# Hybrid encoder block on one core: the feed-forward's first product in seven block products of eight, with the weight sums made in DRAM

## Chip, core and metric

The program runs on one core of one Trainium2 chip. The metric is the device time of one execution in microseconds (us), lower is better. TensorE (PE in the profile) multiplies, VectorE (DVE) and ScalarE (ACT) work elementwise, GpSimd (POOL) fills and masks small tiles, and SyncE (SP) issues the DMAs. Each engine works through its own list of instructions in the order in which the program was emitted.

## The reference, cut to what matters

One layer of a hybrid encoder over 16 + 512 positions with 1024 features: a normed projection, a convolution branch, a gated delta rule with 8 heads, and a feed-forward part. The change is in the feed-forward part alone:

```python
    u2 = rmsnorm(h, norm_ffn_w)
    up = causal_dwconv(u2 @ w_up, ffn_dw_w, ffn_dw_b)        # w_up: 1024 x 5632, three taps per channel
    f_gate, f_val = jnp.split(up, 2, axis=-1)                # 2816 channels each
    return h + (jax.nn.silu(f_gate) * f_val) @ w_down        # w_down: 2816 x 1024
```

## The kernel before

Activations lie with features on the 128 partitions and time along the row: 8 tiles of features, 516 time steps in the last stages. All large products are made in single-precision pieces: an operand x is split into a rounded part hi (ScalarE copies it into the type fp32r) and a rest lo (VectorE subtracts), and a product takes three terms, hi·hi, lo·hi and hi·lo. `weights` (line 449 on) brings one 128 x 1024 weight tile by DMA into one of three `wr` buffers, and splits it into `wh` and `wl`, two buffers each. `gemm` then issues, for 8 feature tiles, 3 terms and 2 halves of time, 48 matmuls of 258 columns into a PSUM tile of the pool `p2` (two buffers).

The program is recorded as a list of operations; `Plan.order` sorts them. It keeps one clock per engine, prices every operation (`price`, line 295), honours buffers (`SLOTS`) and picks for each engine the ready operation of the lowest priority number. `BIAS` shifts the priorities of named groups, `with plan.at(...)` applies them, so a change of the table changes every engine's order in the whole program. All instructions are issued by one line (459), which is why the rows of the profile differ by tile names and not by lines.

Stages in the order of time: projections and convolutions (`glu`), the decay masks of the delta rule (`decays`: a DMA, then an `affine_select` on GpSimd), the triangular inverses (`inverses`, tile `DU`), which `grow` (called for heads 0 to 3 and for heads 4 to 7) assembles into the matrices `Mn`: 16 small copies of diagonal blocks a call on ScalarE, zeros in `LL` from GpSimd, then small matmuls `gP` and `gX`. `heads` runs the recurrence; its `conv4` lets GpSimd clear four columns of a tile `ra` before ScalarE copies the accumulator there. Then the gated branch products (`y`), the output product (`wo`), the second norm, the feed-forward (`up`, `dn`), the final norm.

In the feed-forward, `up(t)` makes one of 44 channel tiles: 48 matmuls on the unnormed `hh`, `hl`, two VectorE multiplications with the norm's row `r` out of PSUM, and three taps (one ScalarE, two VectorE operations). Gate tile t goes through Silu, is multiplied with value tile t, and split into `fh[t]`, `fl[t]`, which the 8 products `dn` read. The residual `hs` stays in SBUF until `dn`.

## Time and profile before

| | |
|---|---|
| median of 3 runs | 1035.56 us (1034.06 to 1035.69) |
| the profiled execution | 1031.66 us, its span 1029.9 us |
| mean granted TensorE clock in it | 0.994 |
| TensorE busy | 1015.1 us, 99% of the span |
| VectorE, ScalarE, GpSimd busy | 717.1, 473.6 and 9.4 us |
| stretch of the product `up` | 639.8 to 894.8 us of the span |
| stretch of the product `dn` | 894.8 to 1010.3 us |

The profile follows one execution. "Busy" is the share of time in which an engine had an instruction under way; the chain of waits follows the last instruction back to whatever released each step; the table by stretches gives busy time, granted clock and DMA load between two times. The mean duration of an instruction contains a tail in which the engine already works at the next one: where starts stand in a row, the distance of two starts is what an instruction costs its engine.

### The profile page before, as it was taken

To read this page: it belongs to the slowest core of one execution; us is meant where nothing else is said; L and a number is where in the kernel's file an instruction comes from. 1 tells how busy PE (TensorE), PEld (TensorE's weight loads), DVE (VectorE), ACT (ScalarE), POOL (GpSimd) and SP (SyncE) were. 2 spreads that over 40 slices of the span, in tenths; PEclk is the share of its full clock that TensorE was granted. 3 is DMA by queue.
4 is the path that set the end of the run, shared out by engine and by line. 5 is a ranking of instruction groups with operands and counts; after the bars stand their busy time and mean duration, and the time that the engine had idled before them with its cause. 6 is when DMAs were issued, how large, how long until landed. Compare 5 with 4: busy or idle time off the path is not lost.

```text
span 1029.9 us, 20012 instructions
## 1 busy us (share of the span) xinstructions
PE 1015.1 (99%) x8430; PEld 973.8 (95%) x8430; DVE 717.1 (70%) x1237; ACT 473.6 (46%) x844; POOL 9.4 (1%) x45
## 2 busy tenths in 40 slices
PE   9998999999999999999999999999999999999996
PEld 7998999998999999999999999999999999988886
DVE  5987999999999999443565555666676767622334
ACT  6777713468545545444373334544434443422222
POOL 0000000000000000000000000000000000000000
PEclk9999999998999999999999999999999999999999
DMA  6243423241212133123214333222232222233332
GB/s 229 76 115 82 128 90 114 83 103 64 73 63 82 53 114 115 62 73 114 93 43 154 128 109 100 85 83 100 86 99 88 86 99 87 93 93 92 97 92 82
DMA packets 44042, 98.40 MB, mean 96 GB/s; under 512 B 12720, under 2 KB 19248, under 8 KB 43952
## 3 DMA queue, kind: packets, MB, share of 16 engines
q1 hardware_dynamic: 43952, 97.12, 29.5%
q8 instruction: 66, 1.08, 0.4%
q14 instruction: 24, 0.20, 0.1%
HBM read 93.89 MB, written 3.21 MB: 94 GB/s over the span
## 4 chain that ended last, share of the span: by engine, by line
PE 93%; DVE 4%; ACT 1%; DMA 1%; issue 0%; SPq 0%; DVEq 0%; ACTq 0%
PE up L459 25%; PE dn L459 12%; PE ga L459 9%; PE y L459 9%; PE q L459 5%; PE v L459 5%; PE z L459 5%; PE wo L459 5%; PE cv L459 4%; PE cg L459 4%; PE o L459 2%; DVE cv L459 1%; PE k L459 1%; PE rs L459 1%; PE S L459 1%; PE qk L459 1%
## 5 line engine op out<-in xcount | busy, mean ns | idle before, releaser
L459 DVE TENSOR_TENSOR wl<-wr,wh 128x1024 fp32r<-128x1024 f32 x157 | 189.2, 1206 | 154.3 <-PE dn L459 59.8
L459 ACT CAST wh<-wr 128x1024 fp32r<-128x1024 f32 x157 | 162.2, 1035 | 257.1 <-PE dn L459 58.2
L459 DVE SCALAR_TENSOR_TENSOR ca<-c,par,ca 128x516 f32<-128x516 f32 (+12 forms) x240 | 176.7, 745 | 3.7 <-ACT ca L459 1.0
L459 PE MATMUL up<-hl,wh 128*128 128x258 f32 x704 | 141.5, 282 | 0.0
L459 PE MATMUL up<-hh,wh 128*128 128x258 f32 x704 | 141.5, 282 | 0.0
L459 PEld LDWEIGHTS up<-hh,wh 128*128 128x128 f32 x704 | 109.2, 190 | 0.2 <-issue 0.2
L459 PEld LDWEIGHTS up<-hl,wh 128*128 128x128 f32 x704 | 108.7, 189 | 0.0
L459 PE MATMUL up<-hh,wl 128*128 128x258 f32 x704 | 92.3, 284 | 0.0
L459 PEld LDWEIGHTS up<-hh,wl 128*128 128x128 f32 x704 | 88.2, 190 | 0.0
L459 PE MATMUL dn<-fh,wh 128*128 128x512 f32 (+1 forms) x198 | 71.6, 370 | 0.0
L459 PE MATMUL dn<-fl,wh 128*128 128x512 f32 (+1 forms) x198 | 71.6, 370 | 0.0
L459 DVE SCALAR_TENSOR_TENSOR uy<-up,par,uy 128x512 f32<-128x512 f32 x88 | 65.9, 749 | 2.8 <-ACT uy L459 1.3
L459 DVE TENSOR_TENSOR up<-up,r 128x258 f32<-128x258 f32 x88 | 33.5, 420 | 47.4 <-PE up L459 44.6
L459 ACT ACTIVATE uy<-up,par 128x512 f32<-128x512 f32 x44 | 35.9, 817 | 55.8 <-DVE up L459 55.8
L459 PE MATMUL ga<-ul,wh 128*128 128x258 f32 (+1 forms) x256 | 58.0, 288 | 0.0
L459 PE MATMUL ga<-uh,wh 128*128 128x258 f32 (+1 forms) x256 | 57.2, 288 | 0.0
L459 DVE SCALAR_TENSOR_TENSOR cv<-ra,par,cv 128x528 f32<-128x528 f32 x69 | 51.7, 765 | 1.4 <-ACT cv L459 1.3
L459 PE MATMUL dn<-fh,wl 128*128 128x512 f32 (+1 forms) x198 | 45.4, 369 | 0.0
L459 PEld LDWEIGHTS dn<-fh,wh 128*128 128x128 f32 x198 | 37.2, 188 | 7.0
L459 PEld LDWEIGHTS dn<-fl,wh 128*128 128x128 f32 x198 | 37.2, 188 | 6.9
L459 PE MATMUL ga<-uh,wl 128*128 128x258 f32 (+1 forms) x256 | 43.1, 286 | 0.0
L459 PEld LDWEIGHTS ga<-ul,wh 128*128 128x128 f32 x256 | 42.2, 190 | 0.6 <-issue 0.4
(284 smaller groups left out, 2194.6 us busy)
## 6 DMA issues: line engine op xcount, KB each, us to landing
wr<-in_win SPq DMA_DIRECT2D x64, 512.0 KB, 3.4
wr<-in_wup SPq DMA_DIRECT2D x44, 512.0 KB, 3.4
wr<-in_wd SPq DMA_DIRECT2D x17, 512.0 KB, 3.5
wr<-in_wdn SPq DMA_DIRECT2D x8, 512.0 KB, 3.5
wr<-in_wco SPq DMA_DIRECT2D x8, 512.0 KB
wr<-in_wo SPq DMA_DIRECT2D x8, 512.0 KB, 3.4
wr<-in_wd SPq DMA_DIRECT2D x8, 384.0 KB, 3.5
x<-in_xT SPq DMA_DIRECT2D x8, 264.0 KB, 5.6
```

Source lines behind the costliest of these rows:

```text
L459: getattr(engines[o.eng], o.fn)(*(get(x) for x in o.a), **{n: get(x) for n, x in o.k.items()})
```

## The change

The 22 gate and 22 value tiles are paired. The first three pairs (`NPRE`) go the old way, 48 matmuls a tile. For the other 19 pairs, the weights of a pair are a 2 x 2 matrix of blocks (even and odd feature tiles by gate and value), the activations a 2 x 2 matrix (even and odd feature tiles by first and second half of time), and `seven` makes the product in seven block products of 12 matmuls each instead of eight. The seven are accumulated into two PSUM tiles of the pool `p1` (four buffers), `sx` and `sz`, in turn; after each product the running sum is read out: `quarters` does this with four ScalarE and three VectorE operations of 258 columns a pair.

The blocks' sums: for the activations `factors` builds them once, on VectorE and ScalarE, right after the second norm, from normed tiles `xn`, in four groups (`nh`, `nl`, `nhl` are their split parts); three more block tiles than before have to be held, so `hs` is written to DRAM (`d_h`) and read back in `dn` (`back`). For the weights `presums` makes the four sums of every pair in DRAM (`ws`): five DMAs a pair issued by GpSimd, two plain copies and three that add to what is there, each group waiting for what it adds to; the first is held behind the last decay mask, and a pair behind the pair two before. A pair's weights are then 3.5 tiles of 128 x 1024 instead of 2.

Beside that: the 32 diagonal copies of `grow` go from ScalarE to GpSimd; the taps get biases of their own (`tp`, `tq`); the planner prices GpSimd's DMAs, and the constants and nearly all entries of `BIAS` are others. No product outside `up` gains or loses a matmul.

```diff
+    def presums(src, n, hold):
+        r = [plan.tile("dram", "con", [P, 4, HD], F32, "ws") for _ in range(n)]
+        for m in range(n):
+          with plan.at(1):
+            h = {hold} | ({softs[-2]} if len(softs) > 1 else set())
+            plan.after = set(h)
+            G.dma_start(out=r[m][:, 0:2], in_=src[:, m, 0:3:2])
+            plan.after = set(h)
+            G.dma_start(out=r[m][:, 2:4], in_=src[:, m, 0:2])
+            G.dma_start(out=r[m][:, 1:3], in_=src[:, m, 3:4].broadcast_to([P, 2, HD]), accum_op=ALU.add)
+            G.dma_start(out=r[m][:, 0], in_=r[m][:, 1], accum_op=ALU.add)
+            G.dma_start(out=r[m][:, 3], in_=r[m][:, 0], accum_op=ALU.add)
+            softs.append(len(plan.ops) - 1)
+        return r
+
+    def seven(src, m, sums, B, w, use):
+        X, Z = p1("sx")[:, :w], p1("sz")[:, :w]
+        flat = lambda v: v.rearrange("p b c -> p (b c)")
+        tiles = (flat(src[:, m, 0:2]), flat(sums[m][:, 0:2]), flat(sums[m][:, 2:4]), src[:, m, 2])
+        for i, (b, to, first, what) in enumerate((('b11', X, True, 'p1'), ('b21', Z, True, 'c11b'),
+                                                  ('t2', X, False, 'u2'), ('t1', Z, True, 'c22b'),
+                                                  ('t3', X, False, 'u3'), ('b22', Z, False, 'c12b'),
+                                                  ('t4', X, False, 'c21'))):
+            if i % 2 == 0:
+                with plan.at("sw"):
+                    hi, lo = weights(tiles[i // 2], D if i < 6 else HD)
+            n, c = len(B), i % 2 * HD
+            runs = [(k, x, y) for part in PARTS for k in range(n) for x, y in ((lo, 0), (hi, 0), (hi, 1))[part]]
+            for j, (k, x, y) in enumerate(runs):
+                PE.matmul(to, lhsT=x[:, c + k * P:c + (k + 1) * P], rhs=B[k][b][y], start=first and j == 0, stop=j == len(runs) - 1,
+                          skip_group_check=not first)
+            use(what, to)
...
+            if what in ('p1', 'u2'):
+                S.copy(out=q(i, j), in_=acc)
+            elif what in ('c22b', 'c21'):
+                S.mul(out=q(i, j), in_=acc, mul=-1.0)
+            else:
+                V.tensor_tensor(out=q(i, j), in0=q(i, j), in1=acc, op=ALU.subtract if i else ALU.add)
...
+    def factors(x0, x1, w, n, hold=None):
...
+        V.tensor_tensor(out=TT[:, 0], in0=X0[:, 0], in1=X0[:, 1], op=ALU.subtract)
+        V.tensor_tensor(out=X0[:, 1], in0=X1[:, 1], in1=X0[:, 1], op=ALU.subtract)
+        V.scalar_tensor_tensor(out=TT[:, 1], in0=TT[:, 0], scalar=-1.0, in1=X1[:, 1], op0=ALU.mult, op1=ALU.subtract)
+        t4 = bt(n=n + "q")
+        V.scalar_tensor_tensor(out=t4[:, :w], in0=TT[:, 1], scalar=-1.0, in1=X1[:, 0], op0=ALU.mult, op1=ALU.subtract)
+        r = {}
+        for v, names in ((X0, ('b11', 't3')), (X1, ('b21', 'b22')), (TT, ('t1', 't2'))):
+            hi, lo = bt(F32R, n + "h"), bt(F32R, n + "l")
+            plan.after = set(hold)
+            S.copy(out=sub(hi), in_=v)
+            V.tensor_tensor(out=sub(lo), in0=v, in1=sub(hi.bitcast(F32)), op=ALU.subtract)
...
-                S.copy(out=Mn[h][r, :, r], in_=D8(h)[r])
+                G.tensor_copy(out=Mn[h][r, :, r], in_=D8(h)[r])
...
+    wus = presums(A['wuq'], FT - NPRE, masks[-1])
     with plan.at(IVP), plan.at("iv"):
         inverses()
...
+        for f in range(0, KT, 2):
+            with plan.at(f"h{f}"):
+                ab = []
+                for i in range(2):
+                    x = bt(n="xn")
+                    for b in range(2):
+                        V.scalar_tensor_tensor(out=x[:, b * 258:(b + 1) * 258], in0=hs[f + i][:, 2 + 256 * b:260 + 256 * b],
+                                               scalar=pc('nf', f + i), in1=r2v[b], op0=ALU.mult, op1=ALU.mult)
+                    ab.append(x)
+                ub.append(factors(*ab, 258, "n"))
...
+    def ffn(t):
+        if t < NPRE:
+            g, v = up(t), up(NPRE + t)
+        else:
+            g, v = quarters(A['wuq'], t - NPRE, wus, ub, 258, "up")
+        with plan.at("tp" if t < NPRE else "tq"):
+            ends(t, g, v)
```

How the order moves, at three places. In a row, the name ahead of the arrow is the tile that is written, behind it what is read; the numbers tell tiles of one name apart; "waits" names the engines or DMA queues (DMAHW from SP, DMASW from GpSimd) whose counters the instruction waits for.

GpSimd before, between the last decay mask and the heads (`LL` is of `grow`, `ra` of `conv4`):

```order
L459 AFFINE_SELECT E_1484<-E_1484 128x512 [waits DMAHW0_49,PE_49]
L459 MEMSET ra_2494 128x4 [waits PE_49]
L459 MEMSET ra_2575 128x4 [waits PE_49]
L459 MEMSET LL_2901 32x8x32 [waits DVE_49]
L459 MEMSET LL_2908 32x8x32 [waits DVE_49,Activation_49,Pool_49]
```

GpSimd now, around the second call of `grow` (`ws` are the weight sums, `mn` the matrices `Mn`); sixteen copies stand here in all:

```order
L469 DMA ws_3014<-in_wuq 128x2x512 [waits DMASW6_49,DMASW0_49]
L469 DMA ws_3058<-in_wuq 128x2x512 [waits DMASW7_49,DMASW1_49]
L469 DMA ws_3014<-ws_3014 128x512 [waits DMASW4_49,DMASW2_49]
L469 MEMSET LL_2617 32x8x32 [waits DVE_49,Activation_49]
L469 MEMSET LL_2625 32x8x32 [waits DVE_49,Activation_49]
L469 COPY mn_1411<-DU_2490 32x4x32
L469 COPY mn_1411<-DU_2490 32x4x32 [waits DMAHW4_49,Pool_49]
L469 DMA ws_3058<-ws_3058 128x512 [waits DMASW5_49,DMASW3_49]
```

Behind them the memsets of `ra` for the remaining heads stand between the DMAs of the later pairs: what GpSimd cleared or masked with nothing ahead of it now stands behind waits for DMAs.

TensorE before, at the seventh tile of `up` (each accumulator is finished by `wl`):

```order
L459 MATMUL up_8395<-hh_7948,wh_8315 128x258 x2
L459 MATMUL up_8395<-hl_7958,wh_8315 128x258 x2
L459 MATMUL up_8395<-hh_7514,wl_8339 128x258 [waits DVE_49]
L459 MATMUL up_8395<-hh_7514,wl_8339 128x258
L459 MATMUL up_8395<-hh_7570,wl_8339 128x258 x2
```

TensorE now, at the same place, shortly after the sixth plain tile (two pairs run interleaved, 8526 with 8536 and 8540 with 8559; `nh_8524`, `nh_8561` and `nl_8565` are of the fourth and last group of `factors`):

```order
L469 MATMUL sz_8536<-nh_8524,wh_8417 128x258 [waits Activation_49]
L469 MATMUL sz_8559<-nh_8432,wh_8500 128x258 [waits PE_49]
L469 MATMUL sz_8559<-nl_8447,wh_8500 128x258
L469 MATMUL sz_8559<-nh_8208,wh_8500 128x258
L469 MATMUL sz_8559<-nl_8223,wh_8500 128x258
L469 MATMUL sz_8559<-nh_8329,wh_8500 128x258
L469 MATMUL sz_8559<-nl_8349,wh_8500 128x258
L469 MATMUL sz_8559<-nh_8524,wh_8500 128x258
L469 MATMUL sx_8526<-nh_8561,wh_8417 128x258 [waits Activation_49]
L469 MATMUL sx_8540<-nh_8561,wh_8500 128x258
L469 MATMUL sz_8536<-nl_8565,wh_8417 128x258 [waits DVE_49]
```

What moved: the block products start on the first three groups and then wait for the fourth.

VectorE before, one pair of `up` tiles:

```order
L459 TENSOR_TENSOR up_9050<-up_8978,r_1_8033 128x258 [waits PE_49]
L459 TENSOR_TENSOR up_9050<-up_8978,r_1_8033 128x258
L459 TENSOR_TENSOR wl_9058<-wr_8874,wh_9024 128x1024 [waits DMAHW1_49]
L459 SCALAR_TENSOR_TENSOR uy_9062<-up_9050,par_82,uy_9062 128x512 [waits Activation_49]
L459 SCALAR_TENSOR_TENSOR uy_9062<-up_9050,par_82,uy_9062 128x512 [waits DVE_49]
L459 TENSOR_TENSOR up_9110<-up_9045,r_1_8033 128x258 [waits PE_49]
L459 TENSOR_TENSOR up_9110<-up_9045,r_1_8033 128x258
L459 TENSOR_TENSOR wl_9119<-wr_8944,wh_9095 128x1024 [waits DMAHW2_49,Activation_49]
L459 SCALAR_TENSOR_TENSOR uy_9122<-up_9110,par_82,uy_9122 128x512 [waits Activation_49]
L459 SCALAR_TENSOR_TENSOR uy_9122<-up_9110,par_82,uy_9122 128x512 [waits DVE_49]
L459 TENSOR_TENSOR uy_9062<-uy_9062,uy_9122 128x512 [waits DVE_49]
L459 TENSOR_TENSOR fl_9172<-uy_9062,fh_9164 128x512 [waits Activation_49]
```

VectorE now, about one pair in the middle of the block products:

```order
L469 TENSOR_TENSOR up_9514<-up_9514,sz_9511 128x258 [waits PE_49,Activation_49]
L469 TENSOR_TENSOR wl_9547<-wr_9451,wh_9528 128x1024 [waits DMAHW3_49,Activation_49]
L469 SCALAR_TENSOR_TENSOR uy_9520<-up_9436,par_69,uy_9520 128x512
L469 SCALAR_TENSOR_TENSOR uy_9520<-up_9436,par_69,uy_9520 128x512 [waits DVE_49]
L469 TENSOR_TENSOR wl_9579<-wr_9501,wh_9564 128x512 [waits DMAHW4_49,PE_49,Activation_49]
L469 TENSOR_TENSOR uy_9487<-uy_9487,uy_9520 128x512 [waits DVE_49]
L469 TENSOR_TENSOR up_9572<-up_9572,sx_9481 128x258 [waits PE_49,Activation_49]
L469 TENSOR_TENSOR fl_9606<-uy_9487,fh_9596 128x512 [waits Activation_49]
L469 TENSOR_TENSOR up_9514<-up_9514,sz_9511 128x258 [waits PE_49]
L469 TENSOR_TENSOR wl_9617<-wr_9535,wh_9603 128x1024 [waits DMAHW5_49,Activation_49]
L469 SCALAR_TENSOR_TENSOR uy_9620<-up_9514,par_69,uy_9620 128x512 [waits Activation_49]
```

What moved: the readings of PSUM, the weight splits and the taps of two pairs stand in turn in one queue.

## Rows read from the trace of the kernel before

**Rows 1.** The chain that ended last, in order of time: start us, us, engine, operation
```profile
639.82 5.97 PE up L459 x49
646.15 3.31 PE up L459 x26
649.46 0.89 PE rc L459 x8
650.35 244.47 PE up L459 x2037
894.82 115.13 PE dn L459 x528
```

**Rows 2.** Busy us of each engine by stretch, granted clock, DMA share, GB/s
```profile
100.00:200.00 100.00, 99.94 (x821) 98.72 (x821) 99.82 (x251) 42.28 (x95) 3.21 (x11) 1.00 0.33 102
700.00:750.00 50.00, 50.00 (x419) 50.00 (x418) 34.65 (x52) 20.75 (x27) 0.00 (x0) 1.00 0.29 96
240.00:250.00 10.00, 10.00 (x156) 9.41 (x157) 9.85 (x19) 8.23 (x22) 0.00 (x0) 0.67 0.32 121
0.00:20.00 20.00, 18.93 (x152) 13.55 (x153) 13.12 (x39) 11.55 (x17) 0.94 (x17) 1.00 0.80 285
```

**Rows 3.** Groups of instructions by shape, 560 to 905 us: busy us, mean ns
```profile
L459 DVE TENSOR_TENSOR wl<-wr,wh 128x1024 fp32r<-128x1024 f32 x59 | 71.9, 1218 | 31.9 <-PE y L459 14.6 <-ACT wh L459 12.8 <-PE wo L459 4.4
L459 ACT CAST wh<-wr 128x1024 fp32r<-128x1024 f32 x59 | 61.5, 1043 | 71.1 <-PE up L459 45.3 <-PE y L459 12.3 <-issue 5.7
L459 ACT ACTIVATE uy<-up,par 128x512 f32<-128x512 f32 x44 | 35.9, 817 | 55.8 <-DVE up L459 55.8
L459 ACT ACTIVATE uy<-uy 128x512 f32<-128x512 f32 x22 | 13.9, 632 | 35.8 <-DVE uy L459 35.8
L459 ACT CAST fh<-uy 128x512 fp32r<-128x512 f32 x22 | 13.5, 616 | 1.9 <-DVE uy L459 1.9
L459 ACT COPY r<-rc 128x258 f32<-128x258 f32 x2 | 0.7, 374 | 3.3 <-PE rc L459 3.3
```

**Rows 4.** VectorE in order of time, inside `up`: start us, us
```profile
700.83 1.53 DVE L459 SCALAR_TENSOR_TENSOR uy<-up,par,uy 128x512 f32<-128x512 f32 x2
702.39 0.69 DVE L459 TENSOR_TENSOR uy<-uy,uy 128x512 f32<-128x512 f32 x1
704.48 0.69 DVE L459 TENSOR_TENSOR fl<-uy,fh 128x512 fp32r<-128x512 f32 x1 [1.40 <-ACT fh L459]
705.09 0.75 DVE L459 TENSOR_TENSOR up<-up,r 128x258 f32<-128x258 f32 x2
705.76 1.22 DVE L459 TENSOR_TENSOR wl<-wr,wh 128x1024 fp32r<-128x1024 f32 x1
706.89 1.53 DVE L459 SCALAR_TENSOR_TENSOR uy<-up,par,uy 128x512 f32<-128x512 f32 x2
```

**Rows 5.** DMA issues: KB each, median us from issue to landing
```profile
wr<-in_wup SPq DMA_DIRECT2D x44, 512.0 KB, 3.4
x<-in_xT SPq DMA_DIRECT2D x8, 264.0 KB, 5.6
out_y<-fin SPq DMA_DIRECT2D x8, 256.0 KB, 2.4
```

**Rows 6.** GpSimd's groups of instructions by shape, whole span
```profile
L459 POOL TENSOR_SCALAR_AFFINE_SELECT E<-E 128x512 f32<-128x512 f32 x8 | 6.1, 759 | 99.6 <-DMA E<-d_g 91.3 <-ACT junk L459 8.3
L459 POOL MEMSET LL<- 32x256 f32 x4 | 1.2, 302 | 85.3 <-DVE c L459 68.3 <-DVE cv L459 17.0
```

**Rows 7.** Instructions of tile `mn`: `grow`'s diagonal copies, min/median/max ns
```profile
L459 ACT COPY mn<-DU x32: 288/295/299, 219.8 to 235.2; 32x128 f32<-32x128 f32 x32
```

**Rows 8.** GpSimd in order of time: the last two masks, last memsets
```profile
108.83 0.63 POOL L459 TENSOR_SCALAR_AFFINE_SELECT E<-E 128x512 f32<-128x512 f32 x1 [8.25 <-ACT junk L459]
112.53 0.63 POOL L459 TENSOR_SCALAR_AFFINE_SELECT E<-E 128x512 f32<-128x512 f32 x1 [3.06 <-DMA E<-d_g]
...
397.92 0.17 POOL L459 MEMSET ra<- 128x4 f32 x3 [41.30 <-ACT v L459]
```

More of the change, by code (lines that the diff above doesn't have):

```diff
@@ L63, in __init__ @@
         self.row = int(np.prod(shape[1:]))
-        self.hist, self.first, self.real, self.left = [], None, None, 0
+        self.hist, self.first, self.real, self.left, self.serial = [], None, None, 0, plan.count
 class Vw:
@@ L242, in at @@
         was = self.late
-        self.prio, self.late = self.prio + by, was or late and by > 0
+        self.prio, self.late = self.prio + by, was or late
         yield
@@ L285, in add @@
         o.act = (args[2].n if writes[0] is args[0] else args[1].n) / 0.6 * o.mode[0] / P if o.mode else o.cost
-        o.tail = 950 + (2800 if fn == "dma_start" and o.lat > 700 and self.run(k) <= P else 0)
+        o.tail = 1300 + (5000 if fn == "dma_start" and o.lat > 700 and self.run(k) <= P else 0)
         if eng == "ACT" and fn == "activation":
@@ L306, in price @@
         if fn == "dma_start":
+            if eng == "POOL":
+                return 1000, int(np.prod(out.shape)) * 4 / 140.0
             return 475, int(np.prod(out.shape)) * 4 / 290.0 * (1 if self.run(k) >= P else 2)
@@ L333, in order @@
         for v in {v for o in ops for v in o.tiles if v.tag in KEEP}:
-            heapq.heappush(line[v.tag], (v.first, id(v), v))
-        table, dma, low, done = None, 0.0, 0, bytearray(len(ops))
+            heapq.heappush(line[v.tag], (v.first, v.serial, v))
+        table, dma, soft, low, done = None, 0.0, 0.0, 0, bytearray(len(ops))
         array = Array()
@@ new lines, in quarters, with use @@
+    def quarters(src, m, sums, B, w, n):
+        c = [bt(n=n), bt(n=n)]
+        q = lambda i, j: c[i][:, j * w:(j + 1) * w]
+        def use(what, acc):
+            i, j = {'p1': (0, 0), 'u2': (0, 1), 'c22b': (1, 1), 'c21': (1, 0),
+                    'c11b': (0, 0), 'c12b': (0, 1), 'u3': (1, 1)}[what]
+            if what in ('p1', 'u2'):
[4 more added lines that the diff above has]
+                V.tensor_tensor(out=q(i, j), in0=q(i, j), in1=acc, op=ALU.subtract if i else ALU.add)
+        seven(src, m, sums, B, w, use)
+        return c
@@ new lines, in factors @@
+    def factors(x0, x1, w, n, hold=None):
+        q = 2 * (w + 2)
+        sub = lambda t: t[:, :q].rearrange("p (b w) -> p b w", b=2)[:, :, :w]
+        two = lambda t: t[:, :2 * w].rearrange("p (b w) -> p b w", b=2)
+        t = bt(n=n + "t")
+        X0, X1, TT = two(x0), two(x1), two(t)
+        hold = set() if hold is None else {hold}
+        plan.after = set(hold)
[7 more added lines that the diff above has]
+            hi, lo = bt(F32R, n + "h"), bt(F32R, n + "l")
+            plan.after = set(hold)
+            S.copy(out=sub(hi), in_=v)
+            V.tensor_tensor(out=sub(lo), in0=v, in1=sub(hi.bitcast(F32)), op=ALU.subtract)
+            for b, nm in enumerate(names):
+                r[nm] = (sub(hi)[:, b], sub(lo)[:, b])
+        hl = bt(F32R, n + "hl")
+        S.copy(out=sub(hl)[:, 0], in_=t4[:, :w])
+        V.tensor_tensor(out=sub(hl)[:, 1], in0=t4[:, :w], in1=sub(hl.bitcast(F32))[:, 0], op=ALU.subtract)
+        r['t4'] = (sub(hl)[:, 0], sub(hl)[:, 1])
+        return r
@@ L1197, in record @@
         sq = s
-    r2v = []
+    d_h = [con([P, SEQ], "d_h", "dram") for _ in range(KT)]
+    for f in range(KT):
+        SY.dma_start(out=d_h[f], in_=hs[f][:, 4:TW])
+    r2v, ub = [], []
     def second_norm():
@@ L1212, in up, with taps3 @@
         u = bt(n="up")
+        for b in range(2):
+            V.tensor_tensor(out=u[:, b * 258:(b + 1) * 258], in0=acc[:, b, :258], in1=r2v[b], op=ALU.mult)
+        return u
+    def taps3(u, t):
         uv = halves(u[:, :516], 258)
-        for b in range(2):
-            V.tensor_tensor(out=uv[:, b], in0=acc[:, b, :258], in1=r2v[b], op=ALU.mult)
         y = bt(n="uy")
@@ L1224, in record, with ends, back @@
     fh, fl = [], []
-    for t in range(FT):
-        g = up(t)
+    def ffn(t):
[5 more added lines that the diff above has]
+            ends(t, g, v)
+    def ends(t, g, v):
+        g = taps3(g, t)
         S.activation(out=g[:, :SEQ], in_=g[:, :SEQ], func=AF.Silu)
-        v = up(FT + t)
+        v = taps3(v, FT + t)
         V.tensor_tensor(out=g[:, :SEQ], in0=g[:, :SEQ], in1=v[:, :SEQ], op=ALU.mult)
-        a, b = split(g[:, :SEQ], SEQ, "f")
+        if t < FT - 3:
+            a, b = split(g[:, :SEQ], SEQ, "f")
+        else:
+            hl = plan.tile("sb", "iv", [P, D], F32R, "fv")
+            a, b = hl[:, :SEQ], hl[:, SEQ:]
+            S.copy(out=a, in_=g[:, :SEQ])
+            V.tensor_tensor(out=b, in0=g[:, :SEQ], in1=a.bitcast(F32), op=ALU.subtract)
         fh.append(a)
         fl.append(b)
+    for t in range(FT):
+        call(ffn, "u", t)
     cuts = ((0, 8), (8, 8), (16, 6))
+    hr = []
+    def back(f):
+        o = bt(n="hr")
+        SY.dma_start(out=o[:, 4:TW], in_=d_h[f])
+        hr.append(o)
+        return o
     def wdown(f, i):
@@ L1253, in record @@
     f, hw, ws = KT - 1, SEQ // 2, {}
-    o, s = hs[f], bt(n="fsq")
+    o, s = back(f), bt(n="fsq")
     for b in range(2):
```

37 lines of the change are left out of this document (26 added, 11 removed).

## The prediction, made before the changed kernel ran

> **What bounds the kernel now.** First the chain of waits in order of time [rows 1]: from 639.8 to 1010 us the end is set by TensorE alone, first by the 2112 matmuls of `up`, then by `dn`. The reader is to see that nothing but TensorE stands there for 370 us: `up` has one gap, at the norm, and the last 2037 of its matmuls take 244.47 us, 0.1200 us each. Then the table by stretches [rows 2]: at 700 to 750 us TensorE is busy for 50.00 of 50 us at full clock, VectorE for 34.65 (69%), ScalarE for 20.75 (42%). So in `up` a matmul less is 0.1200 us less, as long as VectorE, ScalarE and the weight loads, which the change loads more, keep pace. Last the single instructions of these two engines [rows 3, 4].
>
> **What it removes.** 19 pairs of tiles go from 96 to 84 matmuls of the same 258 columns: 228 × 0.1200 = 27.4 us off the path. Six plain tiles (288) and 19 × 84 = 1596 remain. Every matmul still loads its own weights, so I take the same 0.1200 us.
>
> **VectorE and ScalarE in a pair.** A pair now lasts 84 × 0.1200 = 10.08 us. What an instruction costs VectorE is the distance of two starts [rows 4]: a weight split 705.76 to 706.89 = 1.13 us (its mean duration, 1.218 us [rows 3], has a tail under the next one); two taps 700.83 to 702.39 = 1.56; a half's reading from PSUM 0.67 / 2 = 0.335; a 512-column split 0.61. Before, a pair costs 2 × 1.13 + 4 × 0.335 + 2 × 1.56 + 2 × 0.61 = 7.94 us of 48 × 2 × 0.1200 = 11.52, 69%: just what the stretch shows, so the sum can be trusted. Now: 3 × 1.13 + 0.60 for the half tile + 3 × 0.335 + 3.12 + 1.22 = 9.33 us of 10.08, 93%. ScalarE [rows 3]: 3.5 × 1.043 + 4 × 0.374 + 2 × 0.817 + 0.632 + 0.616 = 8.03 us, 80%. Both fit, with little to spare.
>
> Is 93% enough for a queue in which TensorE's accumulators wait? A sum in `sx` must be read out before the product after next may add to it, within 12 × 0.1200 = 1.44 us; behind a weight split that has just begun it takes 1.13 + 0.335 and would be late. The order runs two pairs in turn over four accumulators, so there is mostly another product to go on with. The nearest row is 100 to 200 us [rows 2]: VectorE 99.82 of 100 us busy, TensorE 99.94. Lower bound 0 us. Upper bound by the buffers: four loads a pair through three `wr` buffers leave each 10.08 × 3 / 4 = 7.56 us; 3.4 us to landing [rows 5] + 1.04 + 1.22 = 5.7 us fits, but with the 5.6 us that a load takes in the crowded start it is 7.9, and a pair takes 10.5 us: 19 × 0.45 = 9 us. Rates near full are shown there (285 GB/s [rows 2]), while 3.5 tiles in 10.08 us need 182. I take **+2 us**, near the lower end, since the stretch with the fuller VectorE lost nothing.
>
> **The entry into the block products.** The norm's row is ready about 11 us after `up` begins (650.35 + copy − 639.82 [rows 1]). By the order, VectorE then has ahead of the last group's `nh_8561`: 12 readings (4.0 us), 16 `xn` of 258 columns at about 0.39 (half a tap, 6.2), 17 differences at 0.335 (5.7), 9 splits `nl` at 0.61 (5.5) and 5 weight splits (5.7), 27.1 us; a ScalarE copy of 0.6 follows. TensorE has 288 × 0.12 − 11.3 = 23.3 us of plain matmuls and, by the order, 26 block matmuls (3.1 us): 26.4 us. Short by 1.3 us. Bounds: 0, if the small operations are cheaper than I take them; 5, if a fifth is lost in waits between dependent ones. I take **+2 us**. The taps of the six plain tiles are put off behind all this and cost TensorE nothing: the order ends the block products with about 14 us of VectorE work open (8 taps, 5 weight splits, 4 others), and `dn` has two accumulators of 57 matmuls on earlier tiles to put before the last three, at 115.13 / 528 = 0.218 us [rows 1], 25 us.
>
> **The rest.** `hs` to DRAM and back is 16 DMAs off SP's queue, in stages where 8 loads of weights a stage are hidden; 0. The copies of `grow`: 16 on ScalarE at 0.295 us [rows 7] are 4.7 us a call; on GpSimd a clearing of 32 x 256 takes 0.302 [rows 6], so some 16 × 0.3 = 4.8, and the order has plain matmuls between `gP` and its use. 0, up to 5. Here a rule speaks against the change. From 100 to 200 us VectorE is 99.8% busy [rows 2], mostly with operations on two SBUF inputs. The Trainium skill, "SBUF — State Buffer", section "Who interferes with whom", says that VectorE's instructions with two SBUF inputs and GpSimd's that read SBUF exclude each other through a shared read interface, each holding it to its end. By it each copy could stand behind a tap, and the sum would grow by up to 16 × 0.75 = 12 us a call where no matmuls cover it; no row here has a GpSimd copy beside VectorE.
>
> Elsewhere the tables reorder everything. There is little to win: TensorE idles for 1029.9 − 1015.1 = 14.8 us in all, most of it at the two ends; in the middle the granted clock of 0.67 from 240 to 250 us [rows 2] can be avoided, 10 × 0.33 = 3.3 us, or fall elsewhere. I take 0, range −3 to +5.
>
> **Sum.** 1031.66 − 27.4 + 2 + 2 = 1008.3 us for an execution like the profiled one. That one is 3.9 us below the median of the three runs, so the runs should give **1012 us**; with the bounds, 1003 (−27.4 − 3.3, rounded down) to 1025.
>
> **Rivals.**
> A. VectorE or the loads set the pace of the block products after all: the 9 us above and as much again in late readings of PSUM, 1012 + 16 = 1028 us. For it: 93% by my own sum, one in-order queue for splits, readings and taps. Against: the 99.8% stretch. Still faster.
>
> B. GpSimd's queue falls behind its DMAs; this one ends slower. The sums of the weights are 95 DMAs on GpSimd in ten rounds (two pairs each, the last one), and the zeros and copies that `conv4` and `grow` need stand between them. The round of two pairs has four steps, each waiting for the one before: 2 MB of copies, 1 MB, 0.5 and 0.5 MB of additions. No DMA of this kind is in the trace. Lower bound: 285 GB/s of the start [rows 2] and 1.6 us from the last byte to landing (3.4 less 512 KB at that rate [rows 5]): 7.4 + 3.7 + 1.8 + 1.8 + 4 × 1.6 = 21 us. Upper bound: DRAM is read and written, additions read twice, so twice the transfer: 29.4 + 6.4 = 36 us, and 7 more where weight loads, a third of the DMA engines [rows 2], go at the same time: 43. The time that the order gives a round: the first stands by the seventh mask (108.8 us), the last `ra` in the ninth round, at about 398 us [rows 8]: 289 / 8.7 = 33 us; measured by the second `grow`, some 35. Below that the DMAs are hidden; from there on, each us of a round costs 8.7 us at the end, since VectorE waits for `ra` and TensorE for `Mn`, and with VectorE all weight splits behind. At 40 us a round: 1012 + 5 × 8.7 = 1055 us. Against it: the middle of my bounds, 32, is just hidden, and nothing says that a round is at the upper one. The Trainium skill, "DMA: Bandwidth & Descriptors", section "Anatomy of one DMA — SWDGE (gpsimd) path", prices a DMA from GpSimd at about 2.0 us plus its bytes at 436 GB/s; by that a round is an estimated 18 us and B has next to no chance. No run here shows it.
>
> C. Short waits in `up` lower the clock. At 240 to 250 us the clock stands at 0.67 after stretches of small matmuls although TensorE counts as busy throughout [rows 2]. If a third of the 192 us of block products went so, 64 × 0.33 = 21 us: 1033 us. Against: 1.00 in the other stretches shown, and a mean of 0.994.
>
> D. The new order wins in the middle too, beyond the clock dip: 1000 us.
>
> That the change doesn't remove what it says can be left out: the order has 1884 matmuls in place of 2112.
>
> **Chances.** Forecast 0.67 (1003 to 1025), A 0.08, B 0.19, C 0.02, D 0.04. A measurement of this kernel tells about 0.2% from no change, here 2 us. B begins at 1012 and needs 2.5 us a round over 35 to undo the gain, so 0.03 of it falls near no change and 0.02 below; slower is the remaining 0.14 and half of C, 0.15; faster 0.67 + 0.08 + 0.04 + 0.02 = 0.81; same 0.04. The range goes from 1003 to 1036: it leaves out D and what of B is slower.
>
> **What would show it.** After: `up` has 1884 matmul records at 0.120 us and ends 25 us earlier against its start; VectorE 93% and ScalarE 80% busy there; a wait of TensorE of 1 to 3 us for `nh` or `nl` where the first block products run; no large wait for `sx` or `sz` readings. B would show as TensorE waiting for `Mn` or VectorE for GpSimd between 190 and 400 us, with GpSimd waiting for DMAs, and `up` starting well after 640 us. A round's length is in GpSimd's list. Wrong would be the forecast if `up` costs over 0.125 us a matmul, or if it begins more than 10 us later than now.

## The result

The changed kernel takes **1017.0 us** (median of 4 runs, 1015.08 to 1018.73) against 1034.81 us of the kernel before beside it: ratio 0.983, 95% interval 0.981 to 0.984, 17.8 us less. 1012 us was forecast, with a range of 1003 to 1036.

The chain of the changed kernel in order of time (start us, us, engine, operation), to be held against [rows 1]:

```profile
602.70 46.55 PE wo L469 x384
649.25 5.96 PE up L469 x49
655.56 3.32 PE up L469 x26
...
881.78 115.10 PE dn L469 x528
```

`up` begins at 649.25 us instead of 639.82 and gives way to `dn` at 881.78 instead of 894.82. So its stage lasts 232.5 us in place of 255.0: 22.5 of the 27.4 us saved arrive there. Of these, 9.4 us were given back before the stage began, and what follows `dn`'s start lasts 135.1 us in both. 22.47 − 9.43 = 13.04 us is the difference of the two profiled spans (1029.9 and 1016.9); the medians stand 17.8 us apart, since before's profiled execution was 3 us below its median and after's 1.7 us above.

Where TensorE stood still ahead of `up` is seen in the table by stretches (length, then busy us of TensorE, its weight loads, VectorE, ScalarE, GpSimd; granted clock, share of the transfer engines, GB/s). First before, then after:

```profile
200.00:260.00 60.00, 59.28 (x794) 56.40 (x793) 57.49 (x98) 42.87 (x114) 0.10 (x1) 0.94 0.28 81
260.00:330.00 70.00, 70.00 (x577) 68.73 (x577) 67.54 (x102) 34.48 (x64) 0.44 (x5) 1.00 0.23 73
330.00:400.00 70.00, 69.90 (x619) 67.64 (x617) 67.39 (x103) 35.92 (x73) 0.48 (x6) 1.00 0.30 96
400.00:470.00 70.00, 70.00 (x646) 67.73 (x646) 36.33 (x60) 32.82 (x72) 0.00 (x0) 1.00 0.22 73
```

```profile
200.00:260.00 60.00, 58.71 (x783) 56.33 (x782) 54.77 (x80) 29.07 (x62) 25.20 (x36) 1.00 0.77 170
260.00:330.00 70.00, 67.64 (x558) 64.09 (x558) 62.05 (x99) 35.81 (x83) 17.62 (x28) 0.98 0.82 185
330.00:400.00 70.00, 67.63 (x595) 65.95 (x594) 64.67 (x98) 35.30 (x65) 16.90 (x24) 0.98 0.88 208
400.00:470.00 70.00, 68.04 (x572) 65.23 (x572) 63.93 (x101) 34.11 (x72) 14.23 (x20) 1.00 0.75 170
```

Between 200 and 470 us TensorE idles 8.0 us after and 0.8 before, and the transfer engines are 75 to 88% busy in place of 22 to 30%. The chain there runs through the sums of the weights (`ws`) and through `eg<-d_e`, a row of the delta rule that was written to DRAM and is read back, spread over the partitions:

```profile
229.36 7.91 DMA eg<-d_e
...
267.60 8.60 DMA ws<-in_wuq
277.47 8.63 issue
286.11 6.79 DMA ws<-in_wuq
293.30 5.16 DMA ws<-ws
...
427.18 9.31 DMA eg<-d_e
```

GpSimd's waits, whole span (us in total, times, longest; "issue" is a wait whose cause the profile does not show), and its copies into `mn` by shape:

```profile
POOL ws L469 <- DMA ws<-in_wuq: 136.4, 21, 8.6
POOL ws L469 <- issue: 73.7, 21, 8.0
POOL ws L469 <- DMA ws<-ws: 34.8, 17, 4.2
```

```profile
L469 POOL COPY mn<-DU 32x128 f32<-32x128 f32 x32 | 18.9, 596 | 2.8 <-DMA DU<-d_x 1.6
```

The first round of sums begins at 113.80 us and the tenth at 439.45: 325.65 / 9 = 36.2 us each, so 18 us a pair.

### The profile page after: what moved, and what is told of

It is laid out like the page before. It is cut to its first block, busy times and chain, and to the rows that moved or that the text cites. A ratio compares the mean times of both kernels' runs of the same rounds, so it can differ in the third digit from the quotient of the medians.

```text
span 1016.9 us, 20105 instructions
## 1 busy us (share of the span) xinstructions
PE 995.6 (98%) x8202; PEld 949.7 (93%) x8202; DVE 766.4 (75%) x1304; ACT 526.2 (52%) x945; POOL 108.4 (11%) x172
## 3 DMA queue, kind: packets, MB, share of 16 engines
q0 software_dynamic: 16112, 39.85, 20.4%
## 4 chain that ended last, share of the span: by engine, by line
PE 72%; DMA 12%; issue 6%; DVE 5%; ACT 3%; POOL 1%; SPq 0%; DVEq 0%; ACTq 0%; POOLq 0%
PE dn L469 12%; PE sx L469 10%; PE y L469 9%; DMA ws<-in_wuq 7%; PE sz L469 7%; PE wo L469 5%; PE cv L469 5%; PE ga L469 4%; PE cg L469 4%; PE up L469 3%; PE z L469 2%; PE v L469 2%; DMA ws<-ws 2%; DMA eg<-d_e 2%; PE q L469 2%
## 5 line engine op out<-in xcount | busy, mean ns | idle before, releaser
L469 DVE TENSOR_TENSOR wl<-wr,wh 128x1024 fp32r<-128x1024 f32 (+2 forms) x195 | 225.6, 1158 | 156.0 <-PE dn L469 61.6
L469 ACT CAST wh<-wr 128x1024 fp32r<-128x1024 f32 (+2 forms) x195 | 193.8, 996 | 222.0 <-PE dn L469 56.4
L469 DVE SCALAR_TENSOR_TENSOR ca<-c,par,ca 128x516 f32<-128x516 f32 (+10 forms) x240 | 178.4, 750 | 6.3 <-ACT ca L469 2.3
L469 POOL DMA_DIRECT2D ws<-in_wuq x57 | 49.3, 872 | 151.3 <-DMA ws<-in_wuq 77.7
L469 PE MATMUL sx<-nh,wh 128*128 128x258 f32 x228 | 60.5, 289 | 1.2 <-ACT wh L469 0.9
L469 PE MATMUL sz<-nl,wh 128*128 128x258 f32 x228 | 59.8, 283 | 0.0
L469 PE MATMUL sx<-nl,wh 128*128 128x258 f32 x228 | 59.4, 282 | 0.0
L469 PE MATMUL sz<-nh,wh 128*128 128x258 f32 x228 | 59.4, 283 | 0.0
L469 PE MATMUL sz<-nh,wl 128*128 128x258 f32 x228 | 44.6, 283 | 0.0
L469 PEld LDWEIGHTS sx<-nl,wh 128*128 128x128 f32 x228 | 43.2, 190 | 0.0
```

The costliest lines, as they stand in the source:

```text
L469: getattr(engines[o.eng], o.fn)(*(get(x) for x in o.a), **{n: get(x) for n, x in o.k.items()})
```

## The experiments

Three theories of the loss ahead of `up`: **Q**, GpSimd's other instructions stand behind the sums' waits in its queue; **D**, the sums' traffic slows transfers that the others wait for; **O**, the newly tuned order costs it and the sums nothing. The planner sets every order anew at the smallest edit, so nearly all edits were made behind it, where the ordered list is written out: all instructions keep their places on all engines but for those that a run is about. All ratios are against before; `up`'s start and its stage (to `dn`'s start) are read from each run's chain.

| run | median us | ratio, 95% | `up` begins | stage |
|---|---|---|---|---|
| after | 1017.0 | 0.9827 (0.9811 to 0.9844) | 649.25 | 232.5 |
| e1_no_sums | 1004.3 | 0.9705 (0.9690 to 0.9719) | 635.93 | 231.7 |
| e2_copies_act | 1013.4 | 0.9791 (0.9773 to 0.9809) | 645.71 | 232.6 |
| e3_unchained | 1021.8 | 0.9874 (0.9849 to 0.9900) | 650.67 | 233.0 |
| e4_spread | 1013.8 | 0.9793 (0.9773 to 0.9814) | 642.85 | 233.8 |
| e5_small | 1005.2 | 0.9714 (0.9699 to 0.9728) | 636.39 | 232.3 |
| e6_two_places | 1022.1 | 0.9862 (0.9834 to 0.9890) | 637.13 | 248.7 |
| e7_two_places_act | 1024.5 | 0.9901 (0.9875 to 0.9927) | 640.19 | 247.1 |
| e8_fewer_taps | 1013.8 | 0.9808 (0.9780 to 0.9836) | 644.94 | 231.0 |
| e9_four_places | 1031.7 | 0.9982 (0.9967 to 0.9996) | 661.34 | 235.7 |
| e10_three_places | 1039.0 | 1.0043 (1.0021 to 1.0064) | 661.82 | 242.4 |
| e11_before_copies | 1035.2 | 1.0010 (1.0001 to 1.0020) | 643.01 | 255.0 |
| e12_four_places_later | 1006.3 | 0.9735 (0.9717 to 0.9752) | 635.92 | 233.3 |

**Without the sums.**

```diff
             for i in self.order():
                 o = self.ops[i]
+                if o.eng == "POOL" and o.fn == "dma_start":
+                    continue
...
             softs.append(len(plan.ops) - 1)
+            r[m].tl.real = src.tl.real[:, m]
```

> The changed kernel with the weight sums left out: the 95 transfers of GpSimd that make them are not issued, and the block products load the plain quarter blocks in the places of the sums (the output is therefore not that of the reference). Every other instruction keeps its place on every engine. Theory Q (the time lost ahead of `up` is lost behind the sums' waits in GpSimd's queue) and rival D (it is lost because the sums' traffic slows the other transfers) both expect `up` to begin at 640 to 642 us in the trace instead of 649.25 and the time at about 1008 us. Rival O (the newly tuned order costs it, the sums nothing) expects `up` at 648 to 650 us and 1016 to 1018 us.

1004.3 us. O falls: in the same order `up` begins 13.3 us earlier, TensorE idles 0.03 us between 200 and 470 us, and the clock stands at 1.00:

```profile
200.00:260.00 60.00, 60.00 (x783) 58.05 (x778) 56.49 (x82) 32.24 (x68) 2.07 (x6) 1.00 0.21 68
260.00:330.00 70.00, 69.97 (x593) 66.80 (x591) 65.27 (x106) 36.37 (x84) 0.47 (x6) 1.00 0.24 77
```

The order even gains: `up` begins 3.9 us ahead of before's. So the sums cost 12.7 us by the medians (1017.0 − 1004.3), all of them ahead of `up`.

**An eighth of the bytes, the same chain of waits.**

```diff
...
+            y, z = x[m][:, :, :64], src[:, m, :, :64]
+            for j, (to, of) in enumerate(((y[:, 0:2], z[:, 0:3:2]), (y[:, 2:4], z[:, 0:2]),
+                                          (y[:, 1:3], z[:, 3:4].broadcast_to([P, 2, 64])),
+                                          (y[:, 0], y[:, 1]), (y[:, 3], y[:, 0]))):
+                plan.ops[-5 + j].k.update(out=to, in_=of)
             softs.append(len(plan.ops) - 1)
+            r[m].tl.real = src.tl.real[:, m]
```

> As the run without the sums (the block products load the plain quarter blocks, the output is not that of the reference), but GpSimd issues the 95 transfers again, in their old places and with their chain of waits, each of 64 columns in place of 512 and into a scratch tensor that nothing reads: an eighth of the bytes. Without any sums `up` began at 635.93 us and the time was 1004.3 us; with all of them 649.25 us and 1017.0 us. Theory D (the traffic slows the round trips `eg<-d_e` and `orb<-d_r`, 3.5 and 4.4 us before, 8 to 12 us with the sums) expects nearly all to come back: `up` at 636 to 639 us, 1004 to 1007 us. Theory Q (waits in GpSimd's queue) expects the chain's fixed part to stay, a step of 3 to 5 us in place of 6 to 9 us, so about half of the loss: 641 to 644 us, 1009 to 1012 us.

1005.2 us, `up` at 636.39: within 1 us of no sums at all, though GpSimd issues 95 transfers and waits for them. It is the volume that costs; the number of transfers and steps does not. (Shorter transfers also shorten GpSimd's waits, so this run alone does not part Q from D.) The issue lists, first this run's, then after's (KB each, median us to landing):

```profile
wx<-in_wuq POOLq DMA_DIRECT2D x57, 64.0 KB, 3.2
wx<-wx POOLq DMA_DIRECT2D x38, 32.0 KB, 2.9
```

```profile
ws<-in_wuq POOLq DMA_DIRECT2D x57, 512.0 KB, 7.9
ws<-ws POOLq DMA_DIRECT2D x38, 256.0 KB, 6.1
```

**The volume without the chain.**

```diff
...
+            for j, (to, of) in enumerate(((x[m][:, 1:3], src[:, m, 3:4].broadcast_to([P, 2, HD])),
+                                          (x[m][:, 0], src[:, m, 1]), (x[m][:, 3], src[:, m, 0]))):
+                plan.ops[-3 + j].k = dict(out=to, in_=of)
             softs.append(len(plan.ops) - 1)
```

> The changed kernel with the chain among the sums broken: the three adding transfers of each pair become plain copies of the same sizes out of the weights into a scratch tensor that nothing reads, so GpSimd waits for none of them, but issues as many in the same places (sums are missing, and the output is not that of the reference). Their bytes stay but for the re-reading of what is added to. Every other instruction keeps its place. Theory Q: GpSimd's waits of 6 to 9 us are gone, `up` begins at 640 to 643 us and the time is 1008 to 1011 us. Rival D: the traffic is still there, and denser, `up` at 648 us or later, 1016 us or more. Rival O: 648 to 650 us, 1016 to 1018 us.

1021.8 us, later than after itself: pure Q falls, and D's number is met. With no sum waiting for another, the same bytes came denser, and small transfers of other queues took nearly as long as large ones. GpSimd's queue was not free of waits, though: it stood for 78.6 us at issues (longest 4.8 us), for a cause that the profile does not show. And the loss moved. TensorE idles 3.8 us between 100 and 200 us, where after loses nothing, and 0.03 us between 260 and 400 us, where after, whose chain runs through the sums there, idles 4.7. The chain of this run, then the issue list of before for the same transfers (`orb<-d_r` is a row read back like `eg<-d_e`):

```profile
125.84 7.49 DMA d_m<-mn
...
133.70 9.53 DMA d_m<-mn
...
143.68 7.73 DMA iv<-d_mm
...
233.69 10.90 DMA eg<-d_e
...
377.06 11.07 DMA orb<-d_r
```

```profile
eg<-d_e SPq DMA_DIRECT2D x8, 264.0 KB, 3.5
orb<-d_r SPq DMA_DIRECT2D x8, 258.0 KB, 4.4
...
d_m<-mn SPq DMA_DIRECT2D x32, 16.0 KB, 1.8
```

These results, which go out to DRAM and come back, are on the path however little they are: 16 KB took 7.5 and 9.5 us in place of 1.8. The queue lines of the pages (packets, MB, share of 16 engines' span) tell besides what adding costs; first this run, where all 39.85 MB are plain copies, then after, where half of them add to their target:

```profile
q0 software_dynamic: 11248, 39.85, 13.3%
```

```profile
q0 software_dynamic: 16112, 39.85, 20.4%
```

0.133 × 1018.4 = 135 us of all 16 engines against 0.204 × 1016.9 = 207: half of the bytes at 68 us plain, the other half at 140 when they add, about twice as long (if the plain half costs the same in both runs).

**Copies, and order within GpSimd's queue.**

```diff
+                eng, fn = ("ACT", "copy") if o.eng == "POOL" and o.fn == "tensor_copy" else (o.eng, o.fn)
-                getattr(engines[o.eng], o.fn)(
+                getattr(engines[eng], fn)(
...
```

> The changed kernel with the copies of the diagonal blocks into `mn` back on ScalarE, each at the place in ScalarE's order where GpSimd had it; the sums stay, and every other instruction keeps its place. Theory Q expects that those copies were what stood behind the sums in the two calls of grow: `up` begins 2 to 5 us earlier (644 to 647 us), the time is 1012 to 1015 us, and what stays is lost by the clears of `ra` and `LL`. Rivals D and O expect `up` within 1.5 us of 649 and 1016 to 1018 us.

> The changed kernel with the same sums, but each step of a round of two pairs put into GpSimd's order 13 us (of the planner's time) behind the step before it, so that the sums run until about 640 us instead of 461; every other instruction keeps its place. Theory Q: a step has landed (6 to 9 us) before GpSimd comes to the next, so its other work waits for none; `up` begins at 641 to 645 us, the time is 1009 to 1013 us. Rival D: the traffic is thinner by 526/347, so about a third of the loss comes back ahead of 461 us and some is spread behind it: 646 us, 1014 us. Rival O: 648 to 650 us, 1016 to 1018 us.

The second edit sorts each step of a round to 13 us behind the last:

```diff
...
+            for step, part in enumerate(((0, 1), (2,), (3,), (4,))):
+                put += [(t0 + (n // 10 * 4 + step) * STEP, p[j]) for p in two if p for j in part]
...
+            while put and put[0][0] <= ops[i].t:
+                out.append(put.pop(0)[1])
```

1013.4 and 1013.8 us: each some 3 us better than after, as Q said of the copies (the second interval touches after's). The sums of e4 did not run until 640 us, though: an order is no clock, and where nothing else stood in GpSimd's queue it went on as soon as data allowed; its last transfer was issued at 518.40 us. What it did was to let GpSimd's other work go ahead of a step; the chain then names no GpSimd any more, but still `orb<-d_r` with 10.49 and 7.19 us. So D and Q both have a part. VectorE's waits in after between 200 and 480 us show how large:

```profile
DVE cv L469 <- POOL ra L469: 5.9, 3, 2.8
DVE cv L469 <- DMA eg<-d_e: 3.5, 2, 2.4
DVE orb L469 <- DMA orb<-d_r: 3.2, 1, 3.2
```

It waits 5.9 us for clears that stand in GpSimd's queue (Q) and 6.7 us for round trips (D). Without the sums it waits for neither there; in e3 the round trips alone are left (6.8 us), in e4 one of 2.1 us. That the 12.7 us divide about in half is an estimate from these sums, since not every wait of VectorE reaches TensorE.

**The sums where no round trip is.** Four pairs stay, fifteen move behind the last `orb<-d_r`, for which GpSimd is made to wait:

```diff
...
+        at = out.index(self.gate) + 1
+        return out[:at] + put + out[at:]
...
+                if i == self.gate:
+                    engines["POOL"].tensor_copy(out=self.mark.make(), in_=o.k["out"].make()[0:1, 0:1])
```

> The changed kernel with all of its sums, at two places: the first four pairs where they are, the other fifteen in rounds of three pairs behind the last `orb<-d_r`, which GpSimd waits for (one copy of one element), so from about 475 us. No round trip stands behind that place. Every other instruction keeps its place. Theory D and theory Q expect the loss between 190 and 475 us to come back: `up` at 636 to 640 us; the sums then run at 40 to 45 us a round until about 690 us, into the first block products, whose loads they slow by 0 to 4 us. Time 1004 to 1009 us. If what the sums cost is the same wherever they lie (memory bandwidth shared with the loads of weights), `up` begins at 645 us or later or ends late by as much, and the time stays at 1013 us or more.

Half right: `up` begins at 637.13 us, 12.1 us earlier, but its stage takes 248.7 us, 17.0 more than without sums, where 0 to 4 were expected. Rounds of three pairs took (678.58 − 478.94) / 4 = 49.9 us, 16.6 us a pair. Rounds of two pairs at the same place took 35.3 us (e12 below), so a third pair adds 14.6 us, and only some 6 us of a round are the same whatever it carries: its length is mostly volume, not its four waits. So the sums ran until 730 us, beside the loads of the block products:

```profile
681.62 9.58 DMA wr<-ws
697.84 5.60 DMA wr<-in_wuq
705.79 6.20 DMA wr<-ws
714.42 7.92 DMA wr<-in_wuq
723.81 9.91 DMA wr<-ws
```

Four loads a pair through three buffers leave each 7.56 us, as the prediction had it; three of these five, 7.9 to 9.9 us, don't fit.

The same with the copies on ScalarE (the edit of e2 on that of e6):

> The run before (sums at two places) with the copies of the diagonal blocks into `mn` on ScalarE besides. Behind no transfer, a copy costs 0.5 to 0.8 us on GpSimd in the changed kernel's trace and 0.295 us on ScalarE before: if they hold TensorE up by themselves, this run is 1 to 4 us faster than the one with sums at two places; if they only did behind the sums' waits, the two are within 1.5 us.

2.4 us slower, not faster, and `up` begins 3.1 us later. That the copies stand better on GpSimd (a median of 0.292 us in e6, against 0.295 us on ScalarE [rows 7]) where no sums surround them is likely but not shown: the intervals overlap. In e2, amid the sums, it was the other way. The copies done alone in before's order:

```diff
                 S.copy(out=Mn[h][r, :, r], in_=D8(h)[r])
+                plan.ops[-1].pool = True
...
+                eng, fn = ("POOL", "tensor_copy") if getattr(o, "pool", False) else (o.eng, o.fn)
```

> The kernel before with one part of the change alone: the 32 copies of the diagonal blocks into `mn` run on GpSimd instead of ScalarE, each at the place in GpSimd's order that its place in the whole order gives; every other instruction keeps its place. No sums are made here. In the pair of runs with two places, these copies on ScalarE began `up` 3.1 us later (640.19 against 637.13 us) and with a clock of 0.97 against 1.00 between 200 and 260 us. If that part of the change is worth something by itself, this run is 1.5 to 4 us faster than before (1031 to 1033.5 us) and the granted clock between 200 and 260 us is above 0.94; if the gain ahead of `up` (3.9 us in the run without sums) is the new order's, it is within 1 us of before, or slower.

1.2 us slower than before; the clock between 200 and 260 us stays at 0.94. The gain ahead of `up` is the new order's as a whole, not that of this part alone.

**Less work on VectorE in `up`.**

```diff
             V.scalar_tensor_tensor(out=yv, in0=uv[:, :, j:256 + j], scalar=pc('fw', t * 3 + j), in1=yv,
                                    op0=ALU.mult, op1=ALU.add)
+            plan.ops[-1].skip = j == 0
```

> The changed kernel without the second tap's multiply-add of each of the 44 convolutions behind `up` (the output is not that of the reference): VectorE has about 1.2 us a pair less, 8.1 us of 10.08 us in place of 9.33 us. Every other instruction keeps its place. `up` took 232.5 us there from its first product to the first of `dn`, where 1884 products at 0.1200 us and the rest of the stage as before make 227.7 us: 4.8 us too long. If VectorE's load is what makes the stalls, 3 to 4 of them come back (228.5 to 229.5 us, the time 1013 to 1014 us); if they come from the loads of weights or from ScalarE, or lie in TensorE itself (a block product of 12 at 1.44 to 1.45 us), the stage stays within 1 us of 232.5 us.

The stage takes 231.0 us, 1.5 less. The two stages by stretch, after's first:

```profile
649.25:881.78 232.53, 231.17 (x1902) 228.55 (x1901) 211.26 (x325) 163.24 (x261) 0.00 (x0) 1.00 0.53 165
```

```profile
644.94:875.94 231.00, 230.34 (x1901) 228.43 (x1901) 187.51 (x284) 162.24 (x261) 0.00 (x0) 1.00 0.53 166
```

VectorE has 24 us less to do and TensorE idles 0.66 us in place of 1.36. So VectorE makes at most about a third of the 4.8 us that are missing: the stage takes 231.7 to 233.8 us in the six traces that differ only ahead of it (after, e1 to e5), and 231.0 is not far below. No run here takes loads or ScalarE away. The 4.3 us by which `up` begins earlier in this run, whose code up to there is after's, show how much the collisions ahead of it vary from execution to execution; the median of the time, 1013.8 us, contains them. The 3 us of e2 and e4 are to be read beside that.

**Four places.** Two pairs early, four where they were, two behind the first `grow`'s copies, eleven behind the last `orb<-d_r`; then the same without the early ones.

```diff
...
+        for at, n in ((start, 2), (mask, 4), (grown, 2), (orb, 11)):
...
+            k = out.index(at) + 1
+            out[k:k] = put
```

> The changed kernel with all of its sums in rounds of two pairs at four places: two pairs from 24 us (behind the write to `par` there), four where they were (113 to about 186 us), two behind the first sixteen copies into `mn` (about 195 to 235 us), eleven behind the last `orb<-d_r` (from about 475 us). Every other instruction keeps its place. Theory V (what counts is volume: a pair's sums keep the transfer engines for 18 us wherever they lie, 36 us a round in the trace of after, 54 us for three pairs in the run with two places, and they hurt a round trip or a late load, nothing else): the last eleven take 198 us and end at about 673 us, ahead of the block products; `up` begins at 637 to 640 us, its stage takes 232 to 235 us, the time is 1005 to 1009 us. If the loads of weights in the stages from 475 us on suffer as those of the block products did (17 us in the run with two places), the time stays above 1013 us.

> As the run with four places, without the first one: four pairs where they were, two behind the first sixteen copies into `mn`, thirteen behind the last `orb<-d_r`. Theory V: the last thirteen take 234 us and end at about 710 us, so the sums lie beside the first three or four pairs of block products (from 676 us on), whose loads are late by some us each: `up` at 637 to 640 us, its stage 235 to 241 us, the time 1008 to 1014 us, 2 to 6 us behind the run with four places. If volume beside the block products does not count, the two are equal.

1031.7 and 1039.0 us, far off, for one cause. The third place lies ahead of two clears of `ra`. In e9, GpSimd in order of time, then the waits between 195 and 260 us:

```profile
225.80 0.81 POOL L491 DMA_DIRECT2D ws<-ws  x1 [2.99 <-DMA ws<-ws]
226.65 0.15 POOL L491 MEMSET ra<- 128x4 f32 x2
```

```profile
DVE cv L491 <- POOL ra L491: 24.4, 1, 24.4
...
PE qk L491 <- ACT cv L491: 19.3, 1, 19.3
```

VectorE waits 24.4 us for a clear of 0.1 us, ScalarE behind it, TensorE 19.3 us behind that. Theory Q, pure, at one place. The stage of `up` came out just above what was expected, 235.7 and 242.4 us (232 to 235 and 235 to 241), and longer the more sums lie beside it.

Moving that place behind all copies and three more clears:

```diff
-        grown = [i for i in pool if ops[i].fn == "tensor_copy"][15]
+        grown = pool[pool.index([i for i in pool if ops[i].fn == "tensor_copy"][31]) + 3]
```

> The run with four places once more, with its third place moved: the two pairs that stood behind the first sixteen copies into `mn`, ahead of two clears of `ra`, now stand behind all thirty-two copies and three more clears (from about 212 us; the next clear comes at about 264 us in the run without sums, and the round takes 29 to 36 us). Every other instruction keeps its place. Theory: two things cost, a round's wait ahead of another instruction of GpSimd (a clear of 0.07 us waited 24.4 us there and TensorE 19.6 us of them), and the sums' volume beside round trips and the block products' loads. So the 21 us lost between 200 and 260 us come back but for 0 to 3 us (`eg<-d_e` beside the round), `up` begins at 637 to 640 us, its stage takes 232 to 236 us, the time is 1005 to 1010 us. If the 21 us came from the traffic and not from the queue, most of them stay and the time is above 1020 us.

**1006.3 us, 2.65% below before and 0.9% below the changed kernel, with all sums made.** `up` begins at 635.92 us, as without sums; TensorE idles 0.03 us between 200 and 470 us beside a round of sums there, and its stage takes 233.3 us, 1.6 more than without sums:

```profile
200.00:260.00 60.00, 60.00 (x785) 58.05 (x778) 56.86 (x82) 32.13 (x68) 17.57 (x28) 1.00 0.59 138
...
470.00:600.00 130.00, 129.99 (x1170) 128.85 (x1169) 72.41 (x94) 52.58 (x72) 28.66 (x36) 1.00 0.88 218
600.00:637.00 37.00, 37.00 (x308) 37.00 (x308) 20.14 (x25) 14.08 (x19) 8.22 (x10) 1.00 1.03 288
```

From 470 us to 637 the transfer engines are fuller (88 to 103%) than after's between 200 and 470 us (75 to 88%), and TensorE loses nothing: beside the sums there stand loads of weights and of `x`, issued ahead, and the writing of `d_h`, which is not read before `dn`.

## Why the prediction was right, and where it was not

**The matmuls saved: right.** 1884 products are recorded in place of 2112, their starts 0.120 us apart (median) as before, and the stage is 22.5 us shorter.

**VectorE and ScalarE in a pair: right.** Between 750 and 800 us of after VectorE is busy for 45.23 us (90%; 93% was forecast) and ScalarE for 36.63 (73%; 80%).

**Entry and stalls, +2 and +2: right in sum, not in its parts.** The stage lost 27.4 − 22.5 = 4.9 us. The 1.36 us of idle time are not all of it, since a product's modelled tail covers a short stop; the distances of starts show the rest. In after 36 matmuls start more than 0.15 us behind the one before, 5.1 us in all above 0.120 us each; in before five, 0.4 us, at the norm. After has these too. Only 0.6 us stand where the first block products run. The longest stop there, 0.3 us, is for ScalarE's reading of `sx`, which stood behind a weight split; a wait for `nh` or `nl`, as forecast, is not in the trace. About 4 us stand behind, twice the +2 for stalls. The longest, 0.95 us, follows a load of 5.50 us at 838.99 us; the waits that the profile names in the stage are small and divided:

```profile
PEld sx L469 <- ACT wh L469: 1.4, 2, 0.9
PEld sx L469 <- ACT up L469: 1.0, 4, 0.3
PEld sx L469 <- DVE wl L469: 0.6, 2, 0.4
```

**The middle, taken as 0: wrong, and the step that failed.** It was the sum of two terms of opposite sign, and +9.4 us lies outside the −3 to +5 given for it. The new order wins 3.9 us there, more than the 3.3 us for the clock dip (rival D's mechanism, and e1's 1004.3 us is near D's 1000). That is against before's profiled execution, a fast one (granted clock 0.994, where most others have 0.989 to 0.992); against before's median it is some 7 us, an estimate from the 3.2 us between the two: in e11's trace, an execution of 1035.55 us, `up` begins at 643.01 us and its stage takes 255.0 as in before's. The sums of the weights cost 12.7 us. They are what rival B was about, and its signs were seen: GpSimd waiting for its own transfers, and `up` late (9.4 us; the bound set for a wrong forecast was 10). B's round was put at 21 to 43 us with "32, just hidden" as the middle; it took 36.2, over the budget of 33 to 35. The transfers were sized right: 207 us / 9.5 rounds = 21.8 us of all 16 engines a round, half of the bytes at the plain time and half at twice that, and the middle of the bounds has 22.0 (1.5 times 7.4 + 3.7 + 1.8 + 1.8). The mis-sized term is the rest of a round, 14.4 us in place of 9.9 (four landings, and half of the 7 us for weight loads). GpSimd's 73.7 us at issues, 7.8 us a round, had no term; why it stood there stays open, and some of it may lie beside transfers under way.

B's mechanism was too narrow. It let the sums hurt through GpSimd's queue only, and its price, 8.7 us for each us above 35, gives 10 us, near the 12.7. But about half of VectorE's waits above are for round trips, and the run without the chain lost as much without B's waits, by round trips of 264 KB and of 16 KB that landed after 7 to 11 us. That B's price comes near is luck. The prediction had the row for it, the share of the transfer engines (0.33 and 0.29 in [rows 2]), and used it only to lengthen the round, not the transfers beside it.

The Trainium skill's price in "DMA: Bandwidth & Descriptors", section "Anatomy of one DMA — SWDGE (gpsimd) path" gave an estimated 18 us a round. By the trace it is 36.2: 512 KB land after 7.9 us there, against 3.2 us by the page. 64 KB, with the engines 35 to 49% busy (e5), land after 3.2 us (2.2 by the page). The page also says that a DMA's wait is spent on the engine that issues it; the 24.4 us of e9 show it.

**The copies of `grow`: mis-sized.** 0.3 us each on GpSimd was taken; the mean is 0.596. The Trainium skill's "SBUF — State Buffer", section "Who interferes with whom", spoke for that, and the trace agrees: the slowest stretch has fourteen in 11.12 us, 0.79 each. Nearly every copy that begins while VectorE is in an operation on two SBUF inputs ends about 0.15 us behind that operation (mostly 0.65 to 0.75 us in all behind a tap, 1.18 to 1.31 behind a weight split); beside VectorE's transposes it takes 0.29. But the 12 us a call that the prediction worked out from it didn't come; without sums, with the copies on GpSimd, TensorE idles 0.03 us between 200 and 470 us.

**Why the time still fell inside the forecast's own range:** 27.4 − 4.9 + 3.9 − 12.7 = 13.7 us, next to the 13.0 of the profiled spans, where 23.4 were forecast: 10 us too much. The medians are only 5 us off (1017 for 1012), since the forecast set the median 3.9 us above before's profiled execution, and after's median lies 1.7 us below its own profiled execution: which executions were profiled is luck. That the new order's gain covered a part of the 12.7 us is luck too; neither was forecast. The range itself does not follow from its terms: the bounds given add up to 1004.9 (1035.56 − 27.4 − 3.3) and 1032.2 (1008.2 + 9 + 5 + 5 + 5), not to 1003 and 1025; 1017 lies inside either.

## What to carry to other kernels

A transfer "in the background" was hidden here only where nobody waited for another transfer: before placing bulk traffic, list the stages whose results go out to memory and come back, and put it beside stages that only stream loads issued ahead. On the queue that issues it, put every small instruction that others wait for ahead of the next step, however cheap it is. And test a placement by moving only these instructions in a fixed order; with everything re-planned, a gain of 3.9 us and a loss of 12.7 would have looked like one small number.

## What the runs showed of the hardware

Adding transfers, DRAM to DRAM, held the 16 transfer engines about twice as long per byte as plain copies (207 us against 135 us for 39.85 MB, half of them adding in the first). With the engines full (1.04 of their time from 125 to 144 us in e3) two transfers of 16 KB took 7.5 and 9.5 us to land in place of 1.8. Issuing one transfer of the sums kept GpSimd 0.5 to 1.4 us. At 1.03 of the transfer engines' time and 288 GB/s (e12) TensorE lost nothing as long as its loads were issued ahead. A GpSimd copy of 0.29 us mostly took 0.65 to 0.75 us behind a tap of VectorE and 1.18 to 1.31 behind a weight split.
